# Splitting weights in two steps, the first three of a phase early, and two half units in one PSUM tile: a hybrid decoder step on one core

## The chip, the cores and the metric

The kernel runs on one core of one Trainium2 chip. The metric is the device time of one execution in microseconds (us). A core has five engines with queues of their own: TensorE (PE, matmuls; PEld is its weight load), VectorE (DVE), ScalarE (ACT), GpSimd (POOL) and SyncE (SP, which issues most transfers).

## The reference, cut to what matters

One step of a decoder with two layers: 512 prompt tokens and 8 sample tokens, T = 520 columns, share all weights. Each layer does a mixer with a residual, then a feed-forward net with a residual:

```python
h = _rmsnorm(x) * (1 + sc1) + sh1
mo = mixer(h)                  # h @ w_in ... @ w_out
x = x + g1 * mo
h = _rmsnorm(x) * (1 + sc2) + sh2
fo = _conv_ffn(h, ...)         # silu(conv(h @ w_up)_a) * conv(h @ w_up)_b @ w_down
x = x + g2 * fo
...
y = _rmsnorm(x) * final_g
```

The model has 1024 channels (8 tiles of 128 partitions) and 2816 hidden channels (22 pairs of tiles). The first mixer is a gated MLP beside windowed attention, the second a gated linear recurrence. Everything is fp32.

## The kernel before, in words

Activations are held transposed: 128 channels on the partitions, the 520 tokens along the free dimension, cut in a half of 256 and one of 264 columns (`HALF`).

**Products.** Each fp32 product is made of three products of rounded numbers: `mm3` (L262) multiplies weight-high by activation-high, weight-high by activation-low and weight-low by activation-high. A weight tile of up to 128x1024 is loaded as `wr` (pool of 3, `issue_load`), and `issue_split` (L217) makes its two parts: ACT rounds it into `wh` (L228), DVE subtracts into `wl` (L229). Both pools hold 4 tiles (`WBUFS`).

**Order of the work.** Each engine runs its queue in the order in which the Python code issues. That order is set by generators and a counter: `tick()` is called after each group of matmuls and resumes those tasks whose step has come. `weights()` (L249) hands out the next split weight of the list `stream` and starts a `split_task` (L233) for the one two places on; that task loads ahead (`fill_loads`) and splits both parts in one step, once a pool place is free.

**PSUM.** `psum_pools(3, 2)` leaves three wide tiles of 128x1024 (two banks each, `acc_tile`) and two narrow ones (`bank`). A wide tile goes to the next user when all readers of its last content are done.

**The end of a phase.** `out_final` (L540) makes the output projection of a mixer or FFN. Its last four output tiles are done as eight half units: first the 256 columns of all four (units 0 to 3), then the 264 columns (units 4 to 7). Each unit takes a PSUM tile of its own and issues 24 matmuls (8 channel tiles by 3 products), then `resid` (L522) has DVE add the result to the residual `X` (rows `X<-half` at L95, with two small ones at L528 and L531 where the sample columns are in it), and `ssq` (L442) has ACT square `X` and DVE add the squares. After unit 3 the norm of the first half starts as a task: matmul `ssq` (L468), ACT `sd` (L469), DVE reciprocal (L472), matmul `rb` (L477), then for 8 tiles DVE `nt`, ACT `HH`, DVE `HL` (`h_tiles`, L480). Beside units 5 to 7 the first weights of the next phase are split as well. The next phase starts with `proj_halves` (L306), three tiles at once, first on the first half of the columns.

**The phases.** There are four such ends: out0 into FFN0 (258.8 to 282.5 us), the last down projection of FFN0 into in1 (683 to 707), out1 into FFN1 (851 to 875), and the last down projection of FFN1 (1239 to 1262), after which only the final norm (`final`, L1323) is left. Below they are called the first to the fourth phase end. The `glu_task` (L615) of the FFN and `split_to` (L581) split the gated activations; between in1 and out1 the recurrence runs on DVE (rows `th`, `gt`, `gate`, `yl` around L1144 to L1185).

Of the kernel before, what the change touches and what calls it, by code (L numbers as in the profile page):

```python
# [50 lines left out]
def kernel(ctx: ExitStack, tc: tile.TileContext, I: dict, O: dict):  # L51
    nc = tc.nc
    cp = ctx.enter_context(tc.tile_pool(name="cp", bufs=1))
    wp = ctx.enter_context(tc.tile_pool(name="wp", bufs=1))
    bp = ctx.enter_context(tc.tile_pool(name="bp", bufs=37))
    sp = ctx.enter_context(tc.tile_pool(name="sp", bufs=2))
    ctx.enter_context(tc.manual_schedule())
    psum = {"ctx": None}
# [102 lines left out]
    stream = [("in0", M_Q), ("in0", M_K)] + [("in0", M_V + j) for j in range(4)]  # L161
# [21 lines left out]
            for a in ("k", "v"):  # L183
                copies.append((O["c" + a][b, r0:r1, :], I["c" + a][b, r0 + 1:r1 + 1, :]))

    W, SPLIT = {}, {}
    pos = {"ld": 0, "cp": 0, "use": 0, "sp": 0, "plan": 0, "rel": 0}
    LOAD_AHEAD, SPLIT_AHEAD, RBUFS, WBUFS = 5, 2, 3, 4

    def src(key):  # L190
        kind = key[0]
        base = {"in0": 0, "out0": 20, "in1": 28, "out1": 44}
        if kind in base:
            return I["w8"][base[kind] + key[1]], 8
        if kind == "up":
            return I["w8"][52 + 44 * key[1] + key[2]], 8
        if kind == "gates":
            return I["wg"][key[1]], 8
        _, l, g, m = key
        a, b = GROUPS[g]  # L200
        return I["wd"][l, m, :, a * 128:b * 128], b - a

    def issue_load():
        i = pos["ld"]
        if i >= len(stream):
            return
        ap, n = src(stream[i])
        t = wp.tile([128, 1024], F32, name=nm("wr"), tag="wr", bufs=RBUFS)
        ld(t[:, :n * 128], ap)
        W[i] = (t, n)  # L210
        pos["ld"] += 1
        if stream[i][0] in ("up", "down") and i % 2 == 0 and pos["cp"] < len(copies):
            o, s = copies[pos["cp"]]
            ld(o, s)
            pos["cp"] += 1

    def issue_split():  # L217
        i = pos["sp"]
        if i >= len(stream):
            return  # L220
        t, n = W.pop(i)
        if stream[i][0] == "gates":
            h, l = (wp.tile([128, 1024], F32R, name=nm("wa"), tag="wa", bufs=4) for _ in range(2))
        else:
            h = wp.tile([128, 1024], F32R, name=nm("wh"), tag="wh", bufs=WBUFS)
            l = wp.tile([128, 1024], F32R, name=nm("wl"), tag="wl", bufs=WBUFS)
        w = n * 128
        act.activation(h[:, :w], t[:, :w], AF.Copy)  # L228
        vec.tensor_tensor(l[:, :w], t[:, :w], h[:, :w].bitcast(F32), op=ALU.subtract)  # L229
        SPLIT[i] = (h, l)  # L230
        pos["sp"] += 1

    def split_task(i):  # L233
        yield 1
        fill_loads()
        while i >= pos["rel"] + WBUFS or pos["sp"] < i or (stream[i][0] == "gates" and not ada_rest.done):
            yield 1
        if pos["sp"] <= i:
            issue_split()
        fill_loads()  # L240

    def fill_loads():
        while pos["ld"] < min(pos["use"] + LOAD_AHEAD, pos["sp"] + RBUFS, len(stream)):
            issue_load()

    def used(n):
# [1 line left out]

    def weights():  # L249
        i = pos["use"]  # L250
        while pos["ld"] <= i:
            issue_load()
        while pos["sp"] <= i:
            issue_split()
        pos["use"] += 1
        pos["plan"] = max(pos["plan"], pos["sp"])
        while pos["plan"] <= min(i + SPLIT_AHEAD, len(stream) - 1):
            spawn(split_task(pos["plan"]))
            pos["plan"] += 1
        return SPLIT.pop(i)  # L260

    def mm3(outs, wh, wl, kk, hi, lo, start, stop):  # L262

        c = slice(kk * 128, kk * 128 + 128)
        for n, (w, x) in enumerate(((wh, hi), (wh, lo), (wl, hi))):
            for o, t in outs:
                pe.matmul(o, w[:, c], x[:, t], start=start and n == 0, stop=stop and n == 2)  # L267

    T0, T1 = slice(0, H0), slice(H0, T)

# [3 lines left out]
    def proj(his, los, order=None, n=8):  # L274
        wh, wl = weights()
        ps = acc_tile()
        ks = order or list(range(n))
        for i, k in enumerate(ks):
            mm3(both(ps), wh, wl, k, his[k], los[k], i == 0, i == len(ks) - 1)
            if i == len(ks) - 1:  # L280
                used(1)
            tick()
        return ps
# [46 lines left out]
    def ada_l0_done():  # L330
        return ada_l0[0].done
# [208 lines left out]
    def out_final(his, los, l, vg, n, order, norm):  # L540


        def early(p0):
            resid(whole(p0), l, vg, 0, 0, T)
            ssq(0)

        p = proj2(his, los, order, n, early)[1]
        for m in range(1, 8 - NHALF):
            if m > 1:
                p = proj(his, los, order, n)  # L550
            resid(whole(p), l, vg, m, 0, T)
            ssq(m)
            if psum["wide"] == 2 and ada_l0_done():
                psum_pools(3, 2)
        act_preload(AF.Sqrt)
        ks = order or list(range(n))
        ws = [weights() for _ in range(NHALF)]
        units = [(h, i) for h in range(2) for i in range(NHALF)]
        t = None
        for h, i in units:  # L560
            ps = bank("half") if psum["wide"] == 2 else acc_tile("half")
            w0, w1 = HALF[h]
            for q, k in enumerate(ks):
                mm3([(ps[:, 0:w1 - w0], slice(w0, w1))], ws[i][0], ws[i][1], k, his[k], los[k], q == 0, q == len(ks) - 1)
                if q % 2:
                    tick()
            if h == 1:
                used(1)
            resid(ps[:, 0:w1 - w0], l, vg, 8 - NHALF + i, w0, w1)
            ssq(8 - NHALF + i, w0, w1)  # L570
            if i == NHALF - 1:
                t = spawn(norm(h), 0)
                if h == 0:
                    first = t
        finish(first)
        return t
# [4 lines left out]
    def split_to(v, name):  # L581
        h, l = slot(name + "h", F32R), slot(name + "l", F32R)
        act.activation(h, v, AF.Copy)  # L583
        vec.tensor_tensor(l, v, h.bitcast(F32), op=ALU.subtract)  # L584
        return h, l

# [28 lines left out]
    def glu_task(l, i, pb, box, G, last):  # L615
        yb = yield from ffn_conv(l, i + NPAIR, pb)
        s = slot("fs")
        act.activation(s, box[0], AF.Silu)
        if not last:
            yield 1  # L620
        vec.tensor_tensor(s, s, yb, op=ALU.mult)  # L621
        if not last:
            yield 1
        G[i] = split_to(s, "g")

    def ffn(l, ready, norm, before_last=None):
        for g, (a, b) in enumerate(GROUPS):
# [658 lines left out]
    for g in (1, 2):  # L1286
# [7 lines left out]
                issue_load()  # L1294
        step(g + 1)
        v_part(g)
    issue_split()
    for k in (6, 7):
        qk_part(k)
        part(2, k)  # L1300
# [10 lines left out]
    t = mixer_even(trip_regions, norm_of(0, 1))  # L1311
# [165 lines left out]
```

## Time and profile before

| what | value |
|---|---|
| three runs | 1281.1, 1277.06, 1279.53 us; median 1279.53 |
| profiled execution, its own time | 1275.57 us |
| its span | 1273.8 us |
| PE busy | 1236.5 us, 97% |
| PE weight load busy | 1159.0 us, 91% |
| DVE busy | 717.7 us, 56% |
| ACT busy | 577.4 us, 45% |
| mean granted clock of PE | 0.989 |

The span is the time from the first to the last instruction; the profiled execution's own time is 1.8 us longer. The shares are averages over the span. A granted clock of 1 is the level of 2.4 GHz, 0.5 that of 1.2 GHz.

### The profile page before, as it was taken

Reading aid. Unit: us, or ns where it says so; the run is one execution under the profiler, and the core shown is the slowest. Engines: PE = TensorE matmul, PEld = TensorE weight load, DVE = VectorE, ACT = ScalarE, POOL = GpSimd, SP = SyncE. Lnnn points to the kernel's source line nnn. Section 1 sums busy time; section 2 is a strip of 40 time slices with the busy share of each in tenths; the row PEclk is TensorE's granted clock in tenths of the full one; section 3 lists DMA queues with packets and bytes.
Section 4 is the critical chain, followed back from the end, with each engine's and each line's share of the span. In section 5 each row is a group of like instructions: output and inputs, shape, how many; then the busy total and the mean of one; then the engine's idle time right before and its main releaser. Section 6 shows DMA issues by size and latency. Waiting matters only on the chain.

```text
span 1273.8 us, 24556 instructions
## 1 busy us (share of the span) xinstructions
PE 1236.5 (97%) x10395; PEld 1159.0 (91%) x10395; DVE 717.7 (56%) x1385; ACT 577.4 (45%) x1002; POOL 79.8 (6%) x143
## 2 busy tenths in 40 slices
PE   8999999999999999999999898999999999999997
PEld 5888767798999999999999898998999999999996
DVE  5646557457743555425664877656655555445544
ACT  4434453235531444214453577734642454225434
POOL 0111322201011000010000000000000000000000
PEclk8999999999999999999999999999999999999998
DMA  9643676755688676775454222245447455545322
GB/s 359 246 162 120 206 249 211 271 182 201 240 275 313 232 261 250 259 255 197 151 204 149 84 84 69 61 142 180 149 162 252 149 199 182 199 153 195 120 81 75
DMA packets 54990, 239.76 MB, mean 188 GB/s; under 512 B 7504, under 2 KB 10328, under 8 KB 53856
## 3 DMA queue, kind: packets, MB, share of 16 engines
q1 hardware_dynamic: 36976, 177.37, 40.3%
q0 software_dynamic: 16816, 59.75, 13.5%
q8 instruction: 82, 1.34, 0.4%
q10 hardware_dynamic: 1088, 1.07, 0.3%
q14 instruction: 28, 0.23, 0.1%
HBM read 232.92 MB, written 72.31 MB: 240 GB/s over the span
## 4 chain that ended last, share of the span: by engine, by line
PE 83%; DVE 5%; ACT 5%; issue 4%; DMA 2%; POOL 1%; SPq 0%; DVEq 0%; POOLq 0%; ACTq 0%
PE mm L267 70%; PE half L267 5%; PE ada L421 2%; ACT wh L228 1%; DVE wl L229 1%; DMA wa<-in_wada 1%; DVE nt L95 1%; DVE HL L95 1%; PE pv L749 1%; PE qk L716 1%; PE ada L388 1%; PE pt L737 1%; DMA X<-in_xT 1%; PE ss L814 0%; DMA wr<-in_w 0%
## 5 line engine op out<-in xcount | busy, mean ns | idle before, releaser
L267 PE MATMUL mm<-HH,wh 128*128 128x256 f32 (+1 forms) x1968 | 420.6, 289 | 7.6 <-DVE X L531 7.3
L267 PE MATMUL mm<-HL,wh 128*128 128x256 f32 (+1 forms) x1968 | 411.5, 284 | 0.7 <-DVE HL L95 0.3
L267 PE MATMUL mm<-HH,wl 128*128 128x256 f32 (+1 forms) x1968 | 409.6, 283 | 0.0
L267 PEld LDWEIGHTS mm<-HH,wh 128*128 128x128 f32 x1968 | 310.7, 189 | 35.8 <-issue 21.2
L267 PEld LDWEIGHTS mm<-HL,wh 128*128 128x128 f32 x1968 | 311.6, 189 | 2.3 <-DVE HL L95 1.9
L267 PEld LDWEIGHTS mm<-HH,wl 128*128 128x128 f32 x1968 | 311.7, 189 | 0.0
L229 DVE TENSOR_TENSOR wl<-wr,wh 128x1024 fp32r<-128x1024 f32 (+1 forms) x188 | 224.3, 1199 | 78.1 <-ACT wh L228 77.1
L228 ACT ACTIVATE wh<-wr 128x1024 fp32r<-128x1024 f32 (+1 forms) x188 | 193.2, 1036 | 111.7 <-PE mm L267 103.5
L95 DVE SCALAR_TENSOR_TENSOR fy<-fraw,pk,fy 128x511 f32<-128x511 f32 (+1 forms) x176 | 132.1, 751 | 190.8 <-ACT fy L604 187.7
L603 ACT ACTIVATE fraw<-mm 128x520 f32<-128x520 f32 x88 | 53.2, 604 | 212.6 <-PE mm L267 212.6
L267 PE MATMUL mm<-gh,wh 128*128 128x256 f32 x576 | 116.8, 284 | 0.0
L267 PE MATMUL mm<-gh,wl 128*128 128x256 f32 x576 | 115.9, 283 | 0.0
L267 PE MATMUL mm<-gl,wh 128*128 128x256 f32 x576 | 115.9, 283 | 0.0
L267 PEld LDWEIGHTS mm<-gh,wh 128*128 128x128 f32 x576 | 89.2, 188 | 7.5 <-issue 7.5
L267 PEld LDWEIGHTS mm<-gh,wl 128*128 128x128 f32 x576 | 89.3, 188 | 0.0
L267 PEld LDWEIGHTS mm<-gl,wh 128*128 128x128 f32 x576 | 89.3, 188 | 0.0
L528 DVE TENSOR_TENSOR r<-mm,mod 128x8 f32<-128x8 f32 x48 | 8.0, 167 | 125.7 <-PE mm L267 125.7
L604 ACT ACTIVATE fy<-mm,pk 128x520 f32<-128x520 f32 x88 | 68.7, 781 | 0.0
L583 ACT ACTIVATE gh<-fs 128x520 fp32r<-128x520 f32 x44 | 28.1, 639 | 81.3 <-DVE fs L621 81.3
L376 POOL DMA_DIRECT2D wa<-in_wada x80 | 42.4, 533 | 335.0 <-PE ada L421 221.9
L449 ACT ACTIVATE sq<-X 128x520 f32<-128x520 f32 (+2 forms) x51 | 25.1, 501 | 76.1 <-DVE X L531 52.9
L584 DVE TENSOR_TENSOR gl<-fs,gh 128x520 fp32r<-128x520 f32 x44 | 30.8, 701 | 30.4 <-ACT gh L583 30.3
(280 smaller groups left out, 1473.5 us busy)
## 6 DMA issues: line engine op xcount, KB each, us to landing
wr<-in_w SPq DMA_DIRECT2D x140, 512.0 KB, 3.7
wa<-in_wada POOLq DMA_DIRECT2D x80, 512.0 KB, 5.7
wr<-in_wd SPq DMA_DIRECT2D x32, 512.0 KB, 3.7
wa<-in_wada SPq DMA_DIRECT2D x32, 256.0 KB, 5.4
out_ck<-in_ck SPq DMA_DIRECT2D x8, 1022.0 KB, 6.6
out_cv<-in_cv SPq DMA_DIRECT2D x8, 1022.0 KB, 6.3
sg<-in_kg POOLq DMA_DIRECT2D x16, 384.0 KB, 4.1
sg<-in_vg POOLq DMA_DIRECT2D x12, 512.0 KB, 5.3
```

Of the source, the lines that this page charges most:

```text
L95: vec.scalar_tensor_tensor(out, in0, s, in1, op0=op0, op1=op1)
L228: act.activation(h[:, :w], t[:, :w], AF.Copy)
L229: vec.tensor_tensor(l[:, :w], t[:, :w], h[:, :w].bitcast(F32), op=ALU.subtract)
L267: pe.matmul(o, w[:, c], x[:, t], start=start and n == 0, stop=stop and n == 2)
L376: st(t, I["wada"][n, k])
L388: pe.matmul(ps[32 * c:32 * c + 32, 0:256], cpad[:, k, :], t[:, 256 * c:256 * c + 256], start=k == 0, stop=k == KD - 1)
L421: pe.matmul(ps[c:c + 32, :], cpad[:, k, :], t[:, 512 * h:512 * h + 512], start=k == 0, stop=k == KD - 1)
L449: act.activation(q[:, t0:t1], X[:, k, t0:t1], AF.Square)
L583: act.activation(h, v, AF.Copy)
L584: vec.tensor_tensor(l, v, h.bitcast(F32), op=ALU.subtract)
L603: act.activation(raw, whole(ps), AF.Copy)
L604: act.activation(y, whole(ps), AF.Identity, bias=b[:, f:f + 1], scale=w[:, 2, f:f + 1])
```

## The change

It has four parts.

1. A split is done in two steps: `split_high` issues the ACT rounding, and two ticks later `split_low` issues the DVE subtraction. The places of `wr` are counted by low parts done (`pos["lo"]`).
2. The first three weights of the three next phases (`EARLY`: FFN0, in1, FFN1) are split three places ahead, and into activation slots: four tiles of 128x512 each (`eh`, `el`, two of each) in place of one `wh` and one `wl` of 128x1024. `OWN` counts the weights that use the `wh` pool.
3. In `out_final`, once the pool is three wide, units 2p and 2p+1 share one PSUM tile: the even one uses columns 0 to 511, the odd one 512 to 1023, each a bank.
4. In the FFN, the low part of a gated activation comes a tick after the high part, save for the last of a group (`split_late`).

```diff
+    heads = [stream.index(("up", 0, 0)), stream.index(("in1", 8)), stream.index(("up", 1, 0))]
+    EARLY = {i + q for i in heads for q in range(3)}
+    OWN = [sum(i not in EARLY for i in range(n)) for n in range(len(stream) + 1)]
...
+    def split_parts(i):
+        n = W[i][1] * 128
...
+        if i in EARLY:
+            return [[(slot(s, F32R), slice(512 * q, 512 * q + 512)) for q in range(2)] for s in ("eh", "el")]
+        return [[(wp.tile([128, 1024], F32R, name=nm(s), tag=s, bufs=WBUFS), slice(0, n))] for s in ("wh", "wl")]
+
+    def split_high():
...
+        for d, c in h:
+            act.activation(d[:, 0:c.stop - c.start], t[:, c], AF.Copy)
+        pos["sp"] += 1
+
+    def split_low():
...
+        for (h, c), (l, _) in zip(*SPLIT[i]):
+            w = c.stop - c.start
+            vec.tensor_tensor(l[:, :w], t[:, c], h[:, :w].bitcast(F32), op=ALU.subtract)
+        pos["lo"] += 1
...
     def split_task(i):
         yield 1
         fill_loads()
-        while i >= pos["rel"] + WBUFS or pos["sp"] < i or (stream[i][0] == "gates" and not ada_rest.done):
+        while (i not in EARLY and OWN[i] >= OWN[pos["rel"]] + WBUFS or pos["lo"] < i
+               or (stream[i][0] == "gates" and not ada_rest.done)):
             yield 1
         if pos["sp"] <= i:
-            issue_split()
+            split_high()
+            yield 2
+        if pos["lo"] <= i:
+            split_low()
         fill_loads()
...
-        while pos["ld"] < min(pos["use"] + LOAD_AHEAD, pos["sp"] + RBUFS, len(stream)):
+        while pos["ld"] < min(pos["use"] + LOAD_AHEAD, pos["lo"] + RBUFS, len(stream)):
...
-        while pos["plan"] <= min(i + SPLIT_AHEAD, len(stream) - 1):
+        while pos["plan"] <= min(i + (SPLIT_AHEAD if pos["plan"] not in EARLY else 3), len(stream) - 1):
...
         for h, i in units:
-            ps = bank("half") if psum["wide"] == 2 else acc_tile("half")
+            if psum["wide"] == 2:
+                ps = bank("half")
+            elif i % 2 == 0:
+                two = acc_tile("half")
+                ps = two[:, 0:512]
+            else:
+                ps = two[:, 512:1024]
...
+    def split_late(v, name):
+        h, l = slot(name + "h", F32R), slot(name + "l", F32R)
+        act.activation(h, v, AF.Copy)
+        yield 1
+        vec.tensor_tensor(l, v, h.bitcast(F32), op=ALU.subtract)
+        return h, l
...
-        if not last:
-            yield 1
-        G[i] = split_to(s, "g")
+        if last:
+            G[i] = split_to(s, "g")
+        else:
+            yield 1
+            G[i] = yield from split_late(s, "g")
```

What it does to the queues is seen at three places. The first is PE's queue at the first phase end, where a unit begins: the last matmul of unit 0 and the first of unit 1, the same for units 2 and 3, and for units 6 and 7. The brackets name the engines' semaphores that an instruction waits for. Before:

```order
L267 MATMUL half_3164<-ch_2864,wl_3029 128x256
L267 MATMUL half_3198<-ch_633,wh_3105 128x256 [waits Activation_49]
L267 MATMUL half_3198<-cl_634,wh_3105 128x256
L267 MATMUL half_3198<-ch_633,wl_3106 128x256 [waits DVE_49]
L267 MATMUL half_3227<-ch_2864,wl_3157 128x256
L267 MATMUL half_3256<-ch_633,wh_3160 128x256 [waits DVE_49,Activation_49]
L267 MATMUL half_3375<-ch_2864,wl_3157 128x264
L267 MATMUL half_3430<-ch_633,wh_3160 128x264 [waits DVE_49,PE_49]
```

With the change:

```order
L293 MATMUL half_3164<-ch_2855,wl_3029 128x256
L293 MATMUL half_3164<-ch_633,wh_3105 128x256 [waits DVE_49,Activation_49]
L293 MATMUL half_3164<-cl_634,wh_3105 128x256
L293 MATMUL half_3164<-ch_633,wl_3106 128x256
L293 MATMUL half_3255<-ch_2855,wl_3157 128x256
L293 MATMUL half_3255<-ch_633,wh_3160 128x256 [waits DVE_49,Activation_49]
L293 MATMUL half_3395<-ch_2855,wl_3157 128x264
L293 MATMUL half_3395<-ch_633,wh_3160 128x264 [waits DVE_49]
```

The order of the matmuls is the same. Units 0 and 1 now write one tile, `half_3164`, and the first matmul of unit 1 waits for DVE, where before it waited for ACT alone (the round of `wh_3105`) and the third one for DVE (`wl_3106`). The odd units 3, 5 and 7 have such a wait too.

The second place is DVE's queue while unit 0 and unit 1 run. Before (`X<-half_3164` is the reading of unit 0, `X<-half_3198` that of unit 1):

```order
L229 TENSOR_TENSOR wl_3157<-wr_2856,wh_3156 128x1024 [waits DMAHW7_49,Activation_49]
L229 TENSOR_TENSOR wl_3161<-wr_3032,wh_3160 128x1024 [waits DMAHW0_49,Activation_49]
L95 SCALAR_TENSOR_TENSOR X<-half_3164,mod_99,X 128x256 [waits PE_49]
L456 TENSOR_TENSOR ssq_2979<-ssq_2979,sq_3153 128x520 [waits DVE_49]
L95 SCALAR_TENSOR_TENSOR X<-half_3198,mod_99,X 128x256 [waits PE_49]
L456 TENSOR_TENSOR ssq_2979<-ssq_2979,sq_3196 128x256 [waits DVE_49,Activation_49]
L95 SCALAR_TENSOR_TENSOR X<-half_3227,mod_99,X 128x256 [waits PE_49]
```

With the change (the readings of units 0, 1 and 2 are the rows `X<-half`, in this order):

```order
L243 TENSOR_TENSOR wl_3157<-wr_2898,wh_3156 128x1024 [waits DMAHW7_49,Activation_49]
L243 TENSOR_TENSOR wl_3161<-wr_3046,wh_3160 128x1024 [waits DMAHW0_49,Activation_49]
L243 TENSOR_TENSOR el_3184<-wr_3121,eh_3182 128x512 [waits DMAHW1_49,Activation_49]
L243 TENSOR_TENSOR el_3185<-wr_3121,eh_3183 128x512 [waits Activation_49]
L95 SCALAR_TENSOR_TENSOR X<-half_3164,mod_99,X 128x256 [waits PE_49]
L482 TENSOR_TENSOR ssq_2979<-ssq_2979,sq_3153 128x520 [waits DVE_49]
L243 TENSOR_TENSOR el_3206<-wr_3177,eh_3204 128x512 [waits DMAHW3_49,Activation_49]
L243 TENSOR_TENSOR el_3207<-wr_3177,eh_3205 128x512 [waits Activation_49]
L243 TENSOR_TENSOR el_3233<-wr_3179,eh_3231 128x512 [waits DMAHW4_49,Activation_49]
L243 TENSOR_TENSOR el_3234<-wr_3179,eh_3232 128x512 [waits Activation_49]
L95 SCALAR_TENSOR_TENSOR X<-half_3164,mod_99,X 128x256 [waits PE_49]
L482 TENSOR_TENSOR ssq_2979<-ssq_2979,sq_3212 128x256 [waits DVE_49]
```

Two `el` stand ahead of the reading of unit 0 and four more ahead of that of unit 1. The second and third phase ends have the same rows; the fourth has no `el`, and two `wl` alone stand ahead of the reading of unit 0.

The third place is DVE's queue at the start of out1, in the stretch from 821 us on. `wl_9457` before and `wl_9473` now are the low part of the same weight, the first of out1. Before:

```order
L1144 TENSOR_TENSOR th_9152<-th_9152,gt_9179 128x520
L1146 TENSOR_TENSOR gt_9179<-gt_9150,pk 128x8 [waits DVE_49]
L1147 SCALAR_TENSOR_TENSOR gt_9179<-gt_9150,th_9152 128x512
L1148 TENSOR_TENSOR gt_9179<-gt_9179,th_9152 128x8 [waits DVE_49]
L1185 TENSOR_TENSOR gate_9447<-gate_9447,gt_9122 128x520 [waits Activation_49]
L229 TENSOR_TENSOR wl_9457<-wr_9208,wh_9456 128x1024 [waits DMAHW1_49,PE_49,Activation_49]
L1144 TENSOR_TENSOR th_9225<-th_9225,gt_9233 128x520
L1146 TENSOR_TENSOR gt_9233<-gt_9223,pk 128x8 [waits DVE_49]
L1147 SCALAR_TENSOR_TENSOR gt_9233<-gt_9223,th_9225 128x512
```

With the change:

```order
L1185 TENSOR_TENSOR th_9168<-th_9168,gt_9195 128x520
L1187 TENSOR_TENSOR gt_9195<-gt_9166,pk 128x8 [waits DVE_49]
L1188 SCALAR_TENSOR_TENSOR gt_9195<-gt_9166,th_9168 128x512
L1189 TENSOR_TENSOR gt_9195<-gt_9195,th_9168 128x8 [waits DVE_49]
L1226 TENSOR_TENSOR gate_9463<-gate_9463,gt_9135 128x520 [waits Activation_49]
L1185 TENSOR_TENSOR th_9238<-th_9238,gt_9249 128x520
L1187 TENSOR_TENSOR gt_9249<-gt_9236,pk 128x8 [waits DVE_49]
L1188 SCALAR_TENSOR_TENSOR gt_9249<-gt_9236,th_9238 128x512
L1189 TENSOR_TENSOR gt_9249<-gt_9249,th_9238 128x8 [waits DVE_49]
L616 TENSOR_TENSOR yl_9492<-gate_9463,yh_9491 128x520 [waits Activation_49]
L243 TENSOR_TENSOR wl_9473<-wr_9246,wh_9472 128x1024 [waits DMAHW1_49,PE_49]
```

The low part has moved behind the four rows of the recurrence (L1144 to L1148 before, L1185 to L1189 now) and behind one `yl`.

## Rows read from the trace of the kernel before

Timeline rows give the start in us, the duration in us, engine, line, operation, tiles, shapes, the count of merged instructions, and in brackets the idle time before and its releaser.

**Rows 1.** The page: busy time by engine, and the chain that ended last.

```profile
PE 1236.5 (97%) x10395; PEld 1159.0 (91%) x10395; DVE 717.7 (56%) x1385; ACT 577.4 (45%) x1002; POOL 79.8 (6%) x143
...
PE 83%; DVE 5%; ACT 5%; issue 4%; DMA 2%; POOL 1%; SPq 0%; DVEq 0%; POOLq 0%; ACTq 0%
```

**Rows 2.** Waits of PE, whole span: releaser, us in total, times, longest us.

```profile
PE mm L267 <- DVE X L531: 8.3, 4, 2.4
PE ssq L468 <- DVE ssq L456: 4.9, 4, 2.0
...
PE mm L267 <- DVE wl L229: 3.5, 2, 2.1
```

**Rows 3.** Timeline of PE: first matmul of unit 1, phase ends one, two, four.

```profile
261.64 0.29 PE L267 MATMUL half<-ch,wh 128*128 128x256 f32 x1
...
686.01 0.28 PE L267 MATMUL half<-gh,wh 128*128 128x256 f32 x1
...
1241.73 0.28 PE L267 MATMUL half<-gh,wh 128*128 128x256 f32 x1
```

**Rows 4.** Timeline of DVE there: the two `wl`, then `X<-half` of unit 0.

```profile
262.96 2.36 DVE L229 TENSOR_TENSOR wl<-wr,wh 128x1024 fp32r<-128x1024 f32 x2 [2.47 <-ACT wh L228]
265.24 0.48 DVE L95 SCALAR_TENSOR_TENSOR X<-half,mod,X 128x256 f32<-128x256 f32 x1
...
689.64 0.48 DVE L95 SCALAR_TENSOR_TENSOR X<-half,mod,X 128x256 f32<-128x256 f32 x1
...
1245.35 0.48 DVE L95 SCALAR_TENSOR_TENSOR X<-half,mod,X 128x256 f32<-128x256 f32 x1
```

**Rows 5.** Timeline of ACT and DVE: splits of 520 columns, back to back.

```profile
814.74 2.73 ACT L583 ACTIVATE yh<-gate 128x520 fp32r<-128x520 f32 x5
...
818.61 3.13 DVE L584 TENSOR_TENSOR yl<-gate,yh 128x520 fp32r<-128x520 f32 x5
```

**Rows 6.** Timeline of PE and DVE: units 4, 5 and 7 of the first phase.

```profile
270.20 0.29 PE L267 MATMUL half<-ch,wh 128*128 128x264 f32 x1
...
270.41 0.48 DVE L95 SCALAR_TENSOR_TENSOR X<-half,mod,X 128x256 f32<-128x256 f32 x1 [2.04 <-PE half L267]
...
273.48 0.37 PE L267 MATMUL half<-ch,wh 128*128 128x264 f32 x1
...
274.16 0.48 DVE L95 SCALAR_TENSOR_TENSOR X<-half,mod,X 128x256 f32<-128x256 f32 x1
...
275.02 0.38 PE L477 MATMUL rb<-ident,sd 128*128 128x128 f32 x2
...
277.29 0.87 DVE L95 SCALAR_TENSOR_TENSOR nt<-X,mod,rb 128x256 f32<-128x256 f32 x2
278.34 0.48 DVE L95 SCALAR_TENSOR_TENSOR HL<-nt,mod,HH 128x256 fp32r<-128x256 f32 x1 [0.19 <-ACT HH L490]
...
279.61 0.29 PE L267 MATMUL half<-ch,wh 128*128 128x264 f32 x1
```

**Rows 7.** Timeline: unit 5 of the last phase, and `X<-half` of unit 4.

```profile
1253.61 0.28 PE L267 MATMUL half<-gh,wh 128*128 128x264 f32 x1
...
1254.09 0.47 DVE L95 SCALAR_TENSOR_TENSOR X<-half,mod,X 128x256 f32<-128x256 f32 x1
```

**Rows 8.** Timeline of PE: at the start of FFN0, and at the end.

```profile
286.58 0.55 PE L267 MATMUL mm<-HH,wh 128*128 128x256 f32 x1 [2.42 <-DVE X L531]
...
1264.43 0.72 PE L468 MATMUL ssq<-ones,ssq 128*128 128x1 f32 x5 [1.65 <-DVE ssq L456]
```

**Rows 9.** Windows, PE alone: stretch, PE busy (matmuls), granted clock, DMA.

```profile
286.60:289.30 2.70, 2.70 (x13) 0.50 0.03 6
710.90:714.00 3.10, 3.10 (x26) 1.00 0.00 0
880.00:883.60 3.60, 3.60 (x19) 0.53 0.02 5
```

**Rows 10.** DMA issues: KB each, median us from issue to landing.

```profile
wr<-in_w SPq DMA_DIRECT2D x140, 512.0 KB, 3.7
```

More of the change, by code (lines that the diff above doesn't have):

```diff
@@ L184 @@
                 copies.append((O["c" + a][b, r0:r1, :], I["c" + a][b, r0 + 1:r1 + 1, :]))
-    W, SPLIT = {}, {}
-    pos = {"ld": 0, "cp": 0, "use": 0, "sp": 0, "plan": 0, "rel": 0}
+    heads = [stream.index(("up", 0, 0)), stream.index(("in1", 8)), stream.index(("up", 1, 0))]
+    EARLY = {i + q for i in heads for q in range(3)}
+    OWN = [sum(i not in EARLY for i in range(n)) for n in range(len(stream) + 1)]
+    W, SPLIT, LOW = {}, {}, {}
+    pos = {"ld": 0, "cp": 0, "use": 0, "sp": 0, "lo": 0, "plan": 0, "rel": 0}
     LOAD_AHEAD, SPLIT_AHEAD, RBUFS, WBUFS = 5, 2, 3, 4
@@ L215, in issue_load, with issue_split @@
             pos["cp"] += 1
-    def issue_split():
-        i = pos["sp"]
[L219 to L230, printed above, removed]
-        pos["sp"] += 1
+    def split_parts(i):
+        n = W[i][1] * 128
+        if stream[i][0] == "gates":
+            return [[(wp.tile([128, 1024], F32R, name=nm("wa"), tag="wa", bufs=4), slice(0, n))] for _ in range(2)]
+        if i in EARLY:
+            return [[(slot(s, F32R), slice(512 * q, 512 * q + 512)) for q in range(2)] for s in ("eh", "el")]
+        return [[(wp.tile([128, 1024], F32R, name=nm(s), tag=s, bufs=WBUFS), slice(0, n))] for s in ("wh", "wl")]
+    def split_high():
+        i = pos["sp"]
+        t = W[i][0]
+        SPLIT[i] = h, l = split_parts(i)
+        for d, c in h:
+            act.activation(d[:, 0:c.stop - c.start], t[:, c], AF.Copy)
+        pos["sp"] += 1
+    def split_low():
+        i = pos["lo"]
+        t = W.pop(i)[0]
+        for (h, c), (l, _) in zip(*SPLIT[i]):
+            w = c.stop - c.start
+            vec.tensor_tensor(l[:, :w], t[:, c], h[:, :w].bitcast(F32), op=ALU.subtract)
+        pos["lo"] += 1
+    def issue_split(i):
+        while pos["lo"] <= i:
+            if pos["sp"] == pos["lo"]:
+                while pos["ld"] <= pos["sp"]:
+                    issue_load()
+                split_high()
+            split_low()
     def split_task(i):
@@ L235, in split_task @@
         fill_loads()
-        while i >= pos["rel"] + WBUFS or pos["sp"] < i or (stream[i][0] == "gates" and not ada_rest.done):
+        while (i not in EARLY and OWN[i] >= OWN[pos["rel"]] + WBUFS or pos["lo"] < i
+               or (stream[i][0] == "gates" and not ada_rest.done)):
             yield 1
         if pos["sp"] <= i:
-            issue_split()
+            split_high()
+            yield 2
+        if pos["lo"] <= i:
+            split_low()
         fill_loads()
     def fill_loads():
-        while pos["ld"] < min(pos["use"] + LOAD_AHEAD, pos["sp"] + RBUFS, len(stream)):
+        while pos["ld"] < min(pos["use"] + LOAD_AHEAD, pos["lo"] + RBUFS, len(stream)):
             issue_load()
@@ L250, in weights @@
         i = pos["use"]
[L251 to L254, printed above, removed]
+        issue_split(i)
         pos["use"] += 1
-        pos["plan"] = max(pos["plan"], pos["sp"])
-        while pos["plan"] <= min(i + SPLIT_AHEAD, len(stream) - 1):
+        pos["plan"] = max(pos["plan"], pos["lo"])
+        while pos["plan"] <= min(i + (SPLIT_AHEAD if pos["plan"] not in EARLY else 3), len(stream) - 1):
             spawn(split_task(pos["plan"]))
@@ L262, in mm3 @@
     def mm3(outs, wh, wl, kk, hi, lo, start, stop):
-        c = slice(kk * 128, kk * 128 + 128)
         for n, (w, x) in enumerate(((wh, hi), (wh, lo), (wl, hi))):
+            c = slice(kk * 128, kk * 128 + 128)
+            for t_, s in w:
+                if s.start <= c.start < s.stop:
+                    v = t_[:, c.start - s.start:c.stop - s.start]
             for o, t in outs:
-                pe.matmul(o, w[:, c], x[:, t], start=start and n == 0, stop=stop and n == 2)
+                pe.matmul(o, v, x[:, t], start=start and n == 0, stop=stop and n == 2)
     T0, T1 = slice(0, H0), slice(H0, T)
@@ L1296 @@
         v_part(g)
-    issue_split()
+    issue_split(pos["lo"])
     for k in (6, 7):
```

## The prediction

> **What bounds the kernel now.** I read the page first. PE is busy 97% of the span, and the chain that ended last runs through PE for 83% [rows 1]: the time is PE's work plus the time in which PE stands. So the waits of PE come next. Three groups of them belong to places that the change touches: matmuls that wait for the residual `X` (8.3 us in four waits), the `ssq` matmul that waits for the sum of squares (4.9 us in four), and matmuls that wait for a weight's low part `wl` (3.5 us in two) [rows 2]. The timeline shows where: at the start of FFN0 PE stands 2.42 us until DVE has read the last half units out of PSUM [rows 8]; at the starts of in1 and FFN1 it does the same for as long, and a wait for `ssq` follows in each of the three places; the fourth of these, 1.65 us, is in the final norm [rows 8]. After the first and the third of the three waits the granted clock is at its 1.2 GHz level for a stretch (0.50 and 0.53), after the second it is not [rows 9]. What DVE and ACT do elsewhere is hidden.
>
> **What can be gained.** Pairs of half units in one tile free a wide tile earlier, so the three waits at a phase start should go: 3 x 2.42 = 7.3 us. The splits of three weights leave the norm's stretch of DVE, and `ssq` then is ready before PE asks for it: 4.9 - 1.65 = 3.25 us. The stretches at half clock go with the waits: 1.35 us of the 2.70 and about 1.7 of the 3.60 [rows 9], 3.0 together. Sum: **13.5 us gained**.
>
> **What the pairs cost.** In the queues of the changed program the first matmul of each odd unit waits for DVE, where that of unit 1 waited for none before. The DVE instruction that belongs to its tile is the reading `X<-half` of the even unit just before. So PE cannot start unit 1, 3, 5 or 7 until DVE has read the unit that PE has only just finished. How long it stands is worked out from where that reading lies in DVE's queue (hundredths of a us between engines are left out).
>
> *Unit 1, first phase end.* Before, the reading of unit 0 started at 265.24 us, directly behind two `wl` that had waited for ACT, and nobody needed it [rows 4]. Now two `el` stand ahead of it. An `el` of 512 columns is nearest to the splits of 520 columns, 3.13 us for five, 0.63 each; its rounding takes ACT 2.73 / 5 = 0.55 us and runs beside the `wl` [rows 5]. So the reading starts at 265.24 + 1.25 and lasts 0.48: unit 1 starts at 266.97, not at 261.64 [rows 3], a wait of **5.33 us**. Second phase end: 689.64 + 1.25 + 0.48 - 686.01 = **5.36** [rows 3, 4]; the third repeats it row for row. Fourth, with no `el`: 1245.35 + 0.48 - 1241.73 = **4.10**. Bounds: 4.1 if the `el` came to cost nothing, 5.4 as worked out; I take the latter, as their place in the queue is fixed.
>
> *Unit 3.* DVE is free by then, so only the way there and back counts: DVE started 0.21 us after the next unit's start (270.41 against 270.20) and takes 0.48 [rows 6]: **0.69**. If the last four `el` come late it is up to 1 us more; this goes into the range.
>
> *Unit 5.* The reading of unit 4 lies behind the reciprocal of the first half's norm, and that waits for the `ssq` matmul, which itself stands behind unit 4. Before, this reading ended at 274.16 + 0.48 = 274.64; unit 5 had started at 273.48 [rows 6]: **1.16**. In the fourth phase 1254.09 + 0.47 - 1253.61 = **0.95** [rows 7].
>
> *Unit 7.* The reading of unit 6 lies behind seven `nt` and six `HL`. They can start when `rb` is done (275.02 + 0.38 = 275.40) and run with a pitch of 0.40 (two `nt` in 0.87), 5.2 us, with 0.2 for the first wait for ACT [rows 6]; the reading of unit 5 between them, with its small rows and the sum of squares, is put at 0.9, that of unit 6 at 0.5. Together 6.8 us after `rb`. Unit 7 started 279.61 - 275.40 = 4.2 after it: a wait of **2.6**. Bounds: 0.69 if DVE had caught up, 2.6. In the fourth phase no such rows exist: 0.69.
>
> Sum of a phase end: 5.3 + 0.7 + 1.2 + 2.6 = 9.8, three of them 29.4; the fourth 4.1 + 0.7 + 1.0 + 0.7 = 6.4. **35.8 us lost.**
>
> **The other parts.** At the start of out1 the low parts move behind rows of the recurrence and a `yl` each. Two waits for `wl`, 3.5 us, stand there already [rows 2]; the later one then ends after one more `gate` and `yl` at 0.63 us each [rows 5]: **1.3 us lost**, bounds 0 (the second wait absorbs it) and 3.5 (it doubles). Elsewhere a low part two ticks later costs nothing: the first product with it lies weights ahead, and DVE is idle 44% of the time. The later low part of a gated activation likewise, and the last of a group is left as it was. Loads: `wr` places are now freed by the low part, as before, since both parts were issued together and DVE's came last; a load lands in 3.7 us [rows 10] and is asked for five weights ahead. Twelve small splits in place of three large pairs per phase take nothing from PE.
>
> **The clock.** New waits of 4 to 5 us are longer than the 2.42 us after which the granted clock fell to 0.5 in two of three cases [rows 8, 9]. A fall cost 1.35 and 1.7 us; I take 1.4 for each of the four long waits, 5.6, and for two of the three of 2.6 us, 2.8: **8.4 us lost**, bounds 0 and 9.8.
>
> **Sum.** 35.8 + 1.3 + 8.4 - 13.5 = 32.0 us. Against the profiled execution, 1275.57 us, that is 1307.6 us. That execution lies 4.0 us below the median of the runs, 1279.53, and the forecast is for a median: **1311 us**, 2.5% slower. A measurement of this kernel can tell 0.3%, 3.8 us, from no change.
>
> **The rivals.**
>
> *The pairs do not wait (faster).* The two halves lie in different columns, and the wait for DVE may be for an old count, long reached. For it speaks that unit 3 and unit 7 had a wait for DVE before as well, at no cost; against it, that unit 1 had none and got one just where the tile is shared. Then the 13.5 us stay, less 1.3 at out1 and about 1 us a phase (0 to 2) for `el` ahead of the first half's squares, since the last of them need a load that lands 3.7 us [rows 10] after the `wl` at 262.96 have freed its place [rows 4]: 13.5 - 1.3 - 3 = 9.2, 1270 us. It decides from the point where the reading of the even unit ends before the odd unit's turn. The Trainium skill, "PSUM — Partial Sum Buffer", section "PSUM bank collisions raise a hardware error", asks only that two engines be kept apart by bank and quadrant of partitions; the halves here are two banks, so by that rule no odd unit need wait, and the sum would be this rival's 1270 us. The rows before show no shared tile, so they neither confirm nor deny it; the queue of the changed program shows a wait. Chance 0.06.
>
> *The pairs wait, but briefly.* If DVE read each even unit at once, units 1, 3 and 7 would wait 0.69 and unit 5 1.16: 3 x 3.2 + 3.0 = 12.6 lost against 13.5 gained and 1.3 at out1, no change, 1280 us. Against it: the queue puts `wl`, `el` and `HL` rows ahead of units 0 and 6. Chance 0.04.
>
> *The clock does not fall.* As in the stretch from 710.90 [rows 9]. 1311 - 8.4 = 1303 us. Chance 0.25.
>
> *More is lost.* DVE falls behind at unit 3, the second wait at out1 doubles, and the clock falls after all seven waits: up to 1319 us. Chance 0.12.
>
> **How the numbers follow.** The forecast has 0.53, its own range 1305 to 1316. The lower end of the range takes no fall of the clock (-8.4), unit 7 waiting 0.7 in place of 2.6 (-5.7) and nothing at out1 (-1.3): 1311 - 15.4 = 1296. The upper end is 1318. Faster has the first rival's 0.06, the same the second's 0.04, slower the rest, 0.90.
>
> **What would show it.** In the profile after, PE's waits by `X` grow from 8.3 us to about 36, with 16 waits of an odd unit: four of 4 to 5.4 us at unit 1, three near 2.6 at unit 7. The waits at the starts of FFN0, in1 and FFN1 and the three `ssq` waits are gone. The `wl` waits near 825 us are about 1.3 us longer. The granted clock is at 0.5 after the long waits. The forecast is wrong if unit 1 starts right behind unit 0, or if the waits at unit 7 are below 1 us.

## The result, and the profile after

The changed kernel takes 1315.07 us (median of four runs, 1314.69 to 1315.15), the kernel before 1278.3 us in the same comparison: a ratio of 1.0286, interval 1.0268 to 1.0303. It is slower by 36.8 us. The forecast was 1311 us with a range of 1305 to 1316, so the result lies inside it, 0.9 us below its upper end. The profiled execution took 1315.02 us against 1275.57, 39.4 us more.

The first part of the page of the changed kernel, busy time by engine, answers to [rows 1]:

```profile
PE 1251.1 (95%) x10395; PEld 1173.5 (89%) x10395; DVE 717.5 (55%) x1394; ACT 578.3 (44%) x1011; POOL 79.5 (6%) x143
```

The span is 1313.2 us. PE issues the same 10395 matmuls but is busy 14.6 us longer, and it is not busy for 62.1 us where it was 37.3 before (1273.8 - 1236.5). So the 39.4 us are of two kinds: 24.8 us in which PE stands, and 14.6 us more for the same matmuls. The granted clock accounts for the second kind: read in windows of half a us, it lost 25.5 us of PE's busy time in this execution and 9.7 in that of before (an estimate; some 16 us of difference).

The waits of PE over the whole span (releaser, us in total, times, longest us) answer to [rows 2]:

```profile
PE half L293 <- DVE X L95: 34.9, 16, 5.3
PE mm L293 <- DVE wl L243: 4.9, 2, 4.7
PE mm L293 <- ACT gt L1135: 3.9, 1, 3.9
...
PE ssq L494 <- DVE ssq L482: 1.6, 1, 1.6
...
PE mm L293 <- DVE X L557: 1.0, 1, 1.0
```

The first line is new: 16 waits of a half unit for a reading, 34.9 us. The waits for `X` at the phase starts have gone, 8.3 us to 1.0, and of the four `ssq` waits only the last is left, 4.9 us to 1.6. The two waits for `wl` have grown from 3.5 to 4.9 us, nearly all of it (4.7) now in one of them.

Where the 16 waits stand is in the timeline of PE, here units 1, 3, 5 and 7 of the first phase end and unit 1 of the fourth:

```profile
265.45 0.55 PE L293 MATMUL half<-ch,wh 128*128 128x256 f32 x1 [5.29 <-DVE X L95]
...
274.53 0.35 PE L293 MATMUL half<-ch,wh 128*128 128x256 f32 x1 [0.67 <-DVE X L95]
...
281.93 0.39 PE L293 MATMUL half<-ch,wh 128*128 128x264 f32 x1 [1.07 <-DVE X L95]
...
290.82 0.39 PE L293 MATMUL half<-ch,wh 128*128 128x264 f32 x1 [2.56 <-DVE X L95]
...
1275.59 0.55 PE L293 MATMUL half<-gh,wh 128*128 128x256 f32 x1 [4.09 <-DVE X L95]
```

And this is the timeline of DVE at units 0 and 1, and just ahead of unit 7, to be read beside [rows 4] and [rows 6]:

```profile
261.34 2.36 DVE L243 TENSOR_TENSOR wl<-wr,wh 128x1024 fp32r<-128x1024 f32 x2 [2.46 <-ACT wh L235]
263.62 1.29 DVE L243 TENSOR_TENSOR el<-wr,eh 128x512 fp32r<-128x512 f32 x2
264.82 0.48 DVE L95 SCALAR_TENSOR_TENSOR X<-half,mod,X 128x256 f32<-128x256 f32 x1
...
289.81 0.48 DVE L95 SCALAR_TENSOR_TENSOR HL<-nt,mod,HH 128x256 fp32r<-128x256 f32 x1
290.21 0.16 DVE L554 TENSOR_TENSOR r<-half,mod 128x8 f32<-128x8 f32 x1
290.28 0.48 DVE L95 SCALAR_TENSOR_TENSOR X<-half,mod,X 128x256 f32<-128x256 f32 x1
```

Two `wl`, two `el` and the reading of unit 0 follow each other without a gap; the reading ends at 265.30 and unit 1 starts at 265.45. Before unit 7 the last `HL` is followed by the reading of unit 6, which ends at 290.76; unit 7 starts at 290.82.

The windows, PE alone (stretch, its length, PE busy and matmuls, granted clock, DMA share, GB/s), answer to [rows 9]. They are the stretches behind the waits of unit 1 and unit 7 of the first phase end, behind the wait in in1 and behind the wait at out1:

```profile
265.50:271.00 5.50, 5.50 (x26) 0.50 0.98 381
291.00:294.50 3.50, 3.50 (x19) 0.57 0.00 0
...
794.70:800.00 5.30, 5.30 (x24) 0.50 0.21 44
845.80:851.00 5.20, 5.02 (x21) 0.50 0.53 142
```

After the wait of 5.3 us the clock stays at its 1.2 GHz level for 5.5 us, and 26 matmuls pass where 46 would have. The wait in in1 (for `gt`, 3.94 us) was there before with the same length, 3.93. Before, the clock was low over this window and back at full soon after it:

```profile
778.20:781.00 2.80, 2.80 (x13) 0.50 0.00 0
```

Now it is low for 5.3 us, behind a wait that the change left as long as it was.

### The profile page after: what moved, and what is told of

Same layout as the page of the kernel before. It is cut to its first block, busy times and chain, and to the rows that moved or that the text cites. A ratio compares the mean times of both kernels' runs of the same rounds, so it can differ in the third digit from the quotient of the medians.

```text
span 1313.2 us, 24586 instructions
## 1 busy us (share of the span) xinstructions
PE 1251.1 (95%) x10395; PEld 1173.5 (89%) x10395; DVE 717.5 (55%) x1394; ACT 578.3 (44%) x1011; POOL 79.5 (6%) x143
## 3 DMA queue, kind: packets, MB, share of 16 engines
q10 hardware_dynamic: 1088, 1.07, 0.2%
## 4 chain that ended last, share of the span: by engine, by line
PE 82%; issue 5%; DVE 5%; ACT 4%; DMA 2%; POOL 1%; SPq 0%; DVEq 0%; POOLq 0%; ACTq 0%
PE mm L293 68%; PE half L293 6%; PE ada L447 2%; DMA wa<-in_wada 1%; DVE nt L95 1%; DVE X L95 1%; ACT wh L235 1%; DVE HL L95 1%; PE ada L414 1%; DVE wl L243 1%; PE ada L385 1%; PE pv L790 1%; PE qk L757 1%; PE pt L778 0%; DMA sg<-in_vg 0%
## 5 line engine op out<-in xcount | busy, mean ns | idle before, releaser
L293 PE MATMUL mm<-HH,wh 128*128 128x256 f32 (+1 forms) x1824 | 377.6, 288 | 0.4 <-ACT HH L1280 0.4
L293 PE MATMUL mm<-HL,wh 128*128 128x256 f32 (+1 forms) x1824 | 368.4, 283 | 0.7 <-DVE HL L95 0.7
L293 PE MATMUL mm<-HH,wl 128*128 128x256 f32 (+1 forms) x1824 | 368.1, 283 | 0.0
L293 PEld LDWEIGHTS mm<-HH,wh 128*128 128x128 f32 x1824 | 282.3, 189 | 27.5 <-issue 20.8
L293 PEld LDWEIGHTS mm<-HL,wh 128*128 128x128 f32 x1824 | 283.4, 189 | 1.1 <-DVE HL L95 1.1
L293 PEld LDWEIGHTS mm<-HH,wl 128*128 128x128 f32 x1824 | 283.5, 189 | 0.0
L243 DVE TENSOR_TENSOR wl<-wr,wh 128x1024 fp32r<-128x1024 f32 (+1 forms) x179 | 213.0, 1195 | 38.5 <-ACT wh L235 38.4
L235 ACT ACTIVATE wh<-wr 128x1024 fp32r<-128x1024 f32 (+1 forms) x179 | 183.9, 1034 | 109.0 <-PE mm L293 95.3
L293 PE MATMUL half<-gh,wh 128*128 128x264 f32 (+1 forms) x128 | 40.4, 316 | 15.8 <-DVE X L95 15.8
L293 PEld LDWEIGHTS half<-gh,wh 128*128 128x128 f32 x128 | 27.4, 214 | 17.2 <-issue 11.4
```

The source lines that it names most:

```text
L235: act.activation(d[:, 0:c.stop - c.start], t[:, c], AF.Copy)
L243: vec.tensor_tensor(l[:, :w], t[:, c], h[:, :w].bitcast(F32), op=ALU.subtract)
L293: pe.matmul(o, v, x[:, t], start=start and n == 0, stop=stop and n == 2)
```

## The experiments

All runs are compared with runs of the kernel before on the same chip.

### The parts apart

**No pairs.** The change without its third part:

```diff
-            if psum["wide"] == 2:
-                ps = bank("half")
-            elif i % 2 == 0:
-                two = acc_tile("half")
-                ps = two[:, 0:512]
-            else:
-                ps = two[:, 512:1024]
+            ps = bank("half") if psum["wide"] == 2 else acc_tile("half")
```

> The change without its third part: each half unit has a PSUM tile of its own again; early splits and late low parts stay. Theory (the pairs carry the whole loss): the 16 waits of odd units, 34.9 us, and the stretches at half clock behind them go, and the three waits of 2.42 us at the phase starts stay away too, since the reading of unit 6 now ends 6.8 us after rb, before the next phase asks for its tile; about 1270 us (1266 to 1274). Rival A (the pairs are what removes the 2.42 us waits): these come back, 7.3 us plus half clock, about 1279 us. Rival B (the early and late splits cost time of their own, by the el rows ahead of the readings): above 1283 us.

Measured: 1271.62 us, ratio 0.9948 (0.9934 to 0.9963): 0.5% faster than the kernel before, a small difference but clear of noise. The 16 waits are gone and those at the phase starts do not come back: rival A falls. But three waits that nobody had expected are left in PE's list:

```profile
PE half L293 <- DVE X L95: 6.0, 3, 2.2
```

The timelines of DVE and PE show them (first phase end):

```profile
265.56 1.28 DVE L243 TENSOR_TENSOR el<-wr,eh 128x512 fp32r<-128x512 f32 x2
266.77 0.48 DVE L95 SCALAR_TENSOR_TENSOR X<-half,mod,X 128x256 f32<-128x256 f32 x1
...
268.78 1.29 DVE L243 TENSOR_TENSOR el<-wr,eh 128x512 fp32r<-128x512 f32 x2 [0.93 <-ACT eh L235]
270.74 1.29 DVE L243 TENSOR_TENSOR el<-wr,eh 128x512 fp32r<-128x512 f32 x2 [0.67 <-ACT eh L235]
271.95 0.48 DVE L95 SCALAR_TENSOR_TENSOR X<-half,mod,X 128x256 f32<-128x256 f32 x1
...
272.48 0.39 PE L293 MATMUL half<-ch,wh 128*128 128x264 f32 x1 [1.87 <-DVE X L95]
```

There are three wide tiles, so unit 4 takes the tile of unit 1. The reading of unit 1 stands behind six `el`. The last four of them wait for ACT's `eh`, and these wait 2.87 and 0.50 us for the load of `wr`. The reading ends at 272.43, and unit 4 starts at 272.48 after a wait of 1.87. So what is left of rival B is 6.0 us.

**Pairs alone.** The kernel before with the shared tiles (the lines taken out above) and nothing else:

> The kernel before with the shared tiles alone. Theory: unit 1 waits 4.1 us at each phase end (no el ahead of the reading), units 3 and 5 wait 0.7 and 1.0, and unit 7 waits about 6.8 us in the first three phase ends, since two wl stand ahead of the reading of unit 6 (its end 286.4 us against a turn at 279.6); 44 us of waits, less 7 to 10 gained at the phase starts, plus about 17 of half clock: about 1327 us (1315 to 1335), slower than the whole change. Rival (all three parts cost alike, so the pairs are a third of the loss): about 1291 us.

Measured: 1318.36 us, ratio 1.031 (1.0294 to 1.0325). The list of PE's waits has one line for it:

```profile
PE half L267 <- DVE X L95: 40.0, 16, 5.5
```

Unit 1 waits 4.06 us instead of 5.29, so the two `el` ahead of the reading of unit 0 are worth 1.2 of it. Unit 7 waits 5.5 us in three phase ends, since a `wl` stands between the readings of units 5 and 6 (timelines of DVE and PE, first phase end):

```profile
285.94 0.48 DVE L95 SCALAR_TENSOR_TENSOR X<-half,mod,X 128x256 f32<-128x256 f32 x1
...
287.93 1.23 DVE L229 TENSOR_TENSOR wl<-wr,wh 128x1024 fp32r<-128x1024 f32 x1 [1.09 <-ACT wh L228]
...
292.30 0.47 DVE L95 SCALAR_TENSOR_TENSOR X<-half,mod,X 128x256 f32<-128x256 f32 x1
...
292.83 0.59 PE L267 MATMUL half<-ch,wh 128*128 128x264 f32 x1 [5.47 <-DVE X L95]
```

The expectation of 6.8 us had counted two `wl` there. The first of them, from 282.49 us, ran about half its time while DVE had to wait for `rb` anyway, which was done at 282.98; the rest of the 1.3 us is not accounted for. The time lies in the expected range: pairs alone cost about 40 us. The whole change costs 36.8, so the other parts together gain a little of it back at most (the intervals of the two ratios overlap).

The waits of 2.42 us at the phase starts and the three `ssq` waits are gone in this run too: PE's list has 1.0 us for `X` and 1.6 for `ssq`, as with the whole change.

**Early splits alone.** No pairs, no late low parts (a split is again one step):

```diff
...
         if pos["sp"] <= i:
             split_high()
-            yield 2
...
```

> The second part alone: three weights of a phase split ahead into slots, both parts of a split in one step, no shared tiles. Theory: the phase-start waits and the ssq waits there go (10.5 us and 3 of half clock), the wait at out1 stays as before (3.5 us in all), and the squares of the first half come 1 to 2 us late behind six el, in three places: about 1269 us (1265 to 1274). Rival (the early split only moves the wait from the phase start to the ssq matmul of the first half): about 1278 us, with three ssq waits of 3 us or more.

Measured: 1283.02 us, ratio 1.0029 (1.0012 to 1.0046): 4 us or 0.3% slower. The theory of 1269 us falls, and so does the rival, for the wait is at another place, in DVE's and PE's timelines of the first phase end:

```profile
265.54 1.28 DVE L243 TENSOR_TENSOR el<-wr,eh 128x512 fp32r<-128x512 f32 x2
268.54 1.29 DVE L243 TENSOR_TENSOR el<-wr,eh 128x512 fp32r<-128x512 f32 x2 [1.72 <-ACT eh L235]
271.27 1.29 DVE L243 TENSOR_TENSOR el<-wr,eh 128x512 fp32r<-128x512 f32 x2 [1.44 <-ACT eh L235]
272.48 0.47 DVE L95 SCALAR_TENSOR_TENSOR X<-half,mod,X 128x256 f32<-128x256 f32 x1
...
273.10 0.55 PE L292 MATMUL half<-ch,wh 128*128 128x256 f32 x1 [5.30 <-DVE X L95]
```

With both parts in one step all six `el` stand ahead of the reading of unit 0, and unit 3, which takes the tile of unit 0, waits 5.30 us; in all 15.6 us in three waits. That is more than the gain at the phase starts, which is there as expected (`X` 1.0 us, `ssq` 1.6).

**Late low parts alone.** No pairs, and `EARLY` empty:

> The first and fourth parts alone: the low part two steps behind the rounding, of a gated activation one step, nothing early, no shared tiles. Theory: it costs the longer wait at out1, 1.3 us and as much in half clock, and nothing else: about 1281 us (1278 to 1283), the wait for wl near 4.7 us in one piece. Rival (it frees ACT and DVE of waits for each other and is a gain): below 1276 us.

Measured: 1273.59 us, ratio 0.996 (0.9945 to 0.9974). The wait at out1 is as foreseen, but the run is faster by 5 us, not slower by 2 or 3: the theory falls. The rival's time holds, but its reason is not shown. PE's waits:

```profile
PE ssq L494 <- DVE ssq L482: 7.8, 4, 2.0
PE mm L293 <- DVE X L557: 5.0, 4, 1.4
PE mm L293 <- DVE wl L243: 4.9, 2, 4.7
```

Against [rows 2] the waits for `X` are shorter (1.3 us each instead of 2.42, as the readings now stand ahead of a `wl`), and the `ssq` waits behind them are longer by nearly as much. The sum is no smaller. Two more runs take this apart:

> The kernel before with the first part of the change alone: the low part of a weight two steps behind its rounding. The run with this and the late gated activations took 1273.6 us where 1281 was expected. Theory (the readings of half units pass ahead of wl in DVE's queue at the phase starts, and a wait of 0.9 us in the first mixer goes): nearly all of that gain is here, about 1274 us (1271 to 1276). Rival (the late gated activations make it): about 1280 us.

Measured: 1273.66 us, ratio 0.9959 (0.9944 to 0.9974): the whole effect is in the low parts of the weights.

> The kernel before with the fourth part of the change alone: the low part of a gated activation one step behind its rounding. Theory: no difference, 1278 us (1275 to 1281), as PE has no wait in the FFN. Rival: about 1273 us, the gain of both late parts.

Measured: 1279.13 us, ratio 0.9998 (0.9984 to 1.0011): the gated activations do nothing, as expected. This run is of use in another way. Its profiled execution took 1282.46 us, 6.9 more than that of the kernel before. PE stands 2.4 us longer in it, over half of that in the waits for `ssq` (6.2 us instead of 4.9). The rest is in the page:

```profile
PE 1241.0 (97%) x10395; PEld 1164.3 (91%) x10395; DVE 717.4 (56%) x1385; ACT 577.1 (45%) x1002; POOL 79.5 (6%) x143
```

PE is busy 4.5 us longer with the same matmuls. The windows behind the waits for `ssq` at FFN0 and in1 show it (the first two); the third is the same stretch at in1 in the kernel before:

```profile
292.20:299.40 7.20, 7.20 (x36) 0.53 0.84 291
719.00:726.00 7.00, 6.96 (x33) 0.51 0.50 150
...
716.40:723.40 7.00, 7.00 (x58) 1.00 0.50 150
```

At in1 both kernels have the same two waits ahead of these windows, 2.42 us for `X` and 2.01 or 2.04 for `ssq` 5.5 us later. In one execution 58 matmuls pass in 7 us, in the other 33. So the same waits cost anything from nothing to 3.4 us of clock, from one execution to the next.

Shorter waits of 1.3 us at the phase starts may let the clock fall less often, which would be a cause for the 5 us of the late low parts. The record speaks against the clock as the whole of it: the mean granted clock of 17 executions of the kernel before is 0.985, that of six with the late low parts of the weights 0.987, and 0.002 of the span is some 2.5 us (an estimate). The cause of the rest stays open.

### Where the reading stands

**Early splits spread out.** No pairs; each early split starts two steps later:

```diff
+        if i in EARLY:
+            yield 2
         if pos["sp"] <= i:
             split_high()
             yield 2
```

> As the first experiment (no shared tiles), and each early split starts two steps later, so that DVE's queue has the reading of unit 0, then el el, reading of unit 1, el el, reading of unit 2, el el, reading of unit 3. Theory (what the early splits still cost is the place of el ahead of the readings of units 0 and 1, for whose tiles units 3 and 4 wait): the three waits of about 2 us at unit 4 and the half clock behind them, 5 us, go: about 1261 us (1257 to 1265). Rival (the early splits cost by ACT, DMA or DVE time as such): 1269 us or more, with a wait in another place.

Measured: 1262.06 us, ratio 0.9864 (0.984 to 0.9887). No half unit waits for a reading any more. PE's longest lines are now the wait for `wl` at out1, that for `gt` in in1, which the two new lines do not touch, and `ssq`:

```profile
PE mm L295 <- DVE wl L243: 4.9, 2, 4.7
PE mm L295 <- ACT gt L1131: 3.9, 1, 3.9
PE ssq L496 <- DVE ssq L484: 2.7, 3, 1.6
```

The readings and the `el` now take turns in DVE's queue (timeline of DVE, readings of units 0 and 1 at the first phase end):

```profile
263.25 0.48 DVE L95 SCALAR_TENSOR_TENSOR X<-half,mod,X 128x256 f32<-128x256 f32 x1
...
264.25 1.28 DVE L243 TENSOR_TENSOR el<-wr,eh 128x512 fp32r<-128x512 f32 x2
265.45 0.48 DVE L95 SCALAR_TENSOR_TENSOR X<-half,mod,X 128x256 f32<-128x256 f32 x1
```

The theory holds, in its time too. By the medians this is 15 us faster than the kernel before and 53 faster than the change. It is 9.6 us below the run without pairs. Between the profiled executions, 1273.07 and 1261.89 us, the three waits at unit 4 make 6.0 us of it and PE's busy time, 1237.7 against 1232.5, another 5.2.

**The whole change, spread out.** The same two lines, with the pairs:

> The whole change with the early splits two steps later, as in the run beside it. Theory (the shared tile is the loss; el ahead of the reading of unit 0 is 1.25 us of the 5.3): unit 1 waits 4.1 us instead of 5.3, the other odd units as with the change: about 1310 us (1305 to 1313). Rival (the order of DVE is the loss): below 1290 us.

Measured: 1306.98 us, ratio 1.0221 (1.0192 to 1.0251).

```profile
PE half L295 <- DVE X L95: 31.2, 16, 4.1
```

The waits are 3.7 us less than with the change: three times the 1.2 us of two `el`. PE's busy time is 4.4 us less with it (1246.7 against 1251.1). The rest stays: the `el` are a small part, and the loss comes with the sharing.

DVE's queue still has its part in these 31.2 us. Where nothing stands ahead of the reading, an odd unit waits 0.67 us; 16 such waits would be 10.7 us (an estimate). The other 20 us or so are rows that stand ahead of the readings: the two `wl` before that of unit 0, the norm's rows before those of units 4 and 6. With tiles of their own the odd units did not wait for them.

**Out1 in one step.** As the spread run, and:

```diff
-            yield 2
+            if stream[i][0] != "out1":
+                yield 2
```

> As e5_spread, and the low parts of the weights of out1 in one step with the rounding again. Theory: the wait for wl at the start of out1 is 3.5 us in two pieces instead of 4.7 in one, and the clock falls for a shorter time: 1 to 3 us below e5_spread. Rival (the later low part at out1 is not what costs there): the same time as e5_spread.

Measured: 1261.76 us, ratio 0.9863 (0.9839 to 0.9888), the same as the spread run; the rival holds. The waits did change,

```profile
PE mm L296 <- DVE wl L243: 3.5, 2, 2.1
```

from 4.9 to 3.5 us, and PE was busy 1.7 us less in the profiled executions. But the waits for `ssq` were longer, 4.5 us against 2.7, and the medians differ by 0.3 us, within their spread.

**Far pairs.** The spread run with shared tiles again, but for units 0 and 2, 1 and 3, and so on:

```diff
-        t = None
+        t, two = None, {}
...
-            elif i % 2 == 0:
-                two = acc_tile("half")
-                ps = two[:, 0:512]
+            elif i < 2:
+                two[i] = acc_tile("half")
+                ps = two[i][:, 0:512]
             else:
-                ps = two[:, 512:1024]
+                ps = two[i - 2][:, 512:1024]
```

> As e5_spread, but with shared tiles for units 0 and 2, 1 and 3, 4 and 6, 5 and 7 instead of neighbours. Theory (a shared tile costs only the time by which the reading of its first unit comes after the turn of its second): unit 2 waits 1.2 us at each phase end (reading ends at 265.7 for a turn at 264.5), unit 3 nothing to 1, units 6 and 7 nothing: about 1267 us (1262 to 1274). Rival (a matmul into a bank beside one that DVE reads, or any shared tile, stalls PE): above 1285 us.

Measured: 1266.14 us, ratio 0.9894 (0.9872 to 0.9917).

```profile
PE half L295 <- DVE X L95: 4.9, 4, 1.3
```

These are four waits of 1.23 to 1.25 us, all of unit 2, and no other. In the timelines of DVE and PE unit 2 starts as soon as the reading of unit 0 is done (first phase end):

```profile
263.30 0.48 DVE L95 SCALAR_TENSOR_TENSOR X<-half,mod,X 128x256 f32<-128x256 f32 x1
...
263.93 0.35 PE L295 MATMUL half<-ch,wh 128*128 128x256 f32 x1 [1.25 <-DVE X L95]
```

Units 3, 6 and 7 share tiles with 1, 4 and 5 and never wait. So a shared tile as such did not stall PE here; what costs is that the second user comes before the first one's reading is done. With neighbours that was so at all 16 odd units.

## Why the prediction was right, point by point

*Unit 1.* Forecast 5.33, 5.36 twice and 4.10 us; measured 5.29, 5.28, 5.31 and 4.09. The two `el` were priced at 1.25 us from splits of 520 columns [rows 5], and pairs with no `el` ahead of the reading wait 1.2 us less.

*Units 3, 5 and 7.* Forecast 0.69, 1.16 and 2.6 us; measured 0.67, 1.07 (1.0 in the other two) and 2.56; in the fourth phase end 0.67, 0.88 and 0.65 for 0.69, 0.95 and 0.69. The extra 1 us that was allowed for unit 3 did not come: the last `el` ended at 270.06 us, before unit 1 did. All 16 waits: 35.8 forecast, 34.9 measured.

*Gains.* Waits for `X` 7.3 us forecast and measured, `ssq` 3.25 against 3.3. But these gains do not need the pairs. The waits are gone in the run with pairs alone, in that without pairs and in that with the early splits alone. So the step that pairs "free a wide tile earlier, so the three waits at a phase start should go" may hold, but in this change it was not needed: with the early splits there is no `wl` in the norm's stretch of DVE, and the waits go with tiles of their own as well. The prediction credited the pairs alone with a gain that the early splits bring as well.

*Out1.* 1.3 us forecast, 1.4 measured, but not as it was reckoned: the second wait was to grow, and it was the first that grew, from 2.13 to 4.68 us, while the second shrank from 1.39 to 0.2. That the sum came out was in part luck.

*The clock.* This term was mis-sized. A fall was put at 1.4 us, from the two seen before [rows 9], 8.4 us for six of them and 3.0 us back: 5.4 net. Measured, with the same matmuls, are 14.6 us. All seven waits of 2.5 us and more at odd units are followed by a fall. After the four of 4.1 to 5.3 us the half clock lasts 5.5 us, 2.75 lost each; after the three of 2.6 us about 1.7 is lost. That is 16 us in place of 8.4. The falls after the waits in in1 and at out1 got longer as well, by some 2.5 us together.

The two rows of before came from an execution in which the clock lost little. Its mean granted clock of 0.989 is as high as any of 38 other executions of that kernel reached; most of them were at 0.986 or below. And the run with the late gated activations, with almost the same waits, lost 4.5 us more in PE's busy time.

*Sum.* 24.8 us more of standing (26.6 forecast) and 14.6 us of clock (5.4 forecast): 39.4 against 32.0 of the profiled executions, 1315 against 1311 us of the medians. The median was met more closely because the forecast added 4.0 us, the gap between profiled execution and median before; afterwards there is no such gap (1315.02 and 1315.07). That covered about half of what the clock term lacked, and was not meant to. The prediction also names a second, wider range, 1296 to 1318; only its lower end is worked out there.

*Rivals.* That the pairs do not wait is refuted by 16 waits; that they wait briefly, by the seven of 2.5 to 5.3 us among them. By the Trainium skill, "PSUM — Partial Sum Buffer", section "PSUM bank collisions raise a hardware error", two engines in two banks need no wait for each other. Here they were held apart all the same, since the program's wait is for the reading of the tile, whatever the bank. No run let PE and DVE into one shared tile at once, so that rule of the Trainium skill was not tried. That the clock does not fall is refuted too: the one case without a fall in [rows 9] stood behind a wait of 2.42 us and said nothing of longer ones. That more is lost came true in one of its three parts, the clock, which fell after all seven long waits; unit 3 waited no longer than forecast, and the waits at out1 did not double.

## What to carry to other kernels

When two users share a buffer, ask when the second one's turn comes and when the first one's reader is done in its own queue; neighbours gave a wait at each of 16 steps, 31.2 us, and users two places apart four short ones, 4.9 us. Before an early task is moved into a queue, list what now stands behind it: the early splits alone, ahead of the readings that free a tile, made this kernel 4 us slower; standing between those readings they belong to the version that is 15 us faster. Price a stall of TensorE with its clock, and take that price from several executions, not from one.

## What the runs showed of the hardware

The granted clock is the unexpected part. In the changed kernel it fell to its 1.2 GHz level behind every wait of PE of 2.5 us and more at a half unit, in in1 and at out1. The low stretch lasted a little over 3 us behind the waits of 2.6 us (0.57 over 3.5 us) and 5.2 to 5.5 us behind those of 3.9 to 5.3 us. Yet behind the wait of 3.9 us in the kernel before it lasted 2.8 us, and in the run with late gated activations it lasted for nearly all of 7.2 us (0.53) behind an `ssq` wait of 2.03 us, shorter than all of these, with a wait of 2.4 us some 5 us earlier.

Even within one execution equal waits had unequal prices. In the run with pairs alone unit 1 waits 4.06 us at the first phase end and 4.07 at the fourth; these are the windows behind them:

```profile
265.50:271.00 5.50, 5.50 (x33) 0.69 1.01 359
...
1276.90:1282.40 5.50, 5.50 (x26) 0.50 0.01 3
```

The first lost 1.7 us, the second 2.75. So the length of the wait alone does not set the price.
